# Mixer of a hybrid decoder trunk: low weight parts behind the second norm's root, forget gate's products and fold apart, norm product and one copy moved

## The chip, the cores and the metric

The kernel runs on one core of one Trainium2 chip. The metric is the device time of one execution in microseconds (us), the median of several runs. The core has five engines with a queue of instructions each: TensorE (PE, matrix products, with its weight loads shown as PEld), VectorE (DVE), ScalarE (ACT), GpSimd (POOL) and SyncE (SP, which here issues the DMAs of the weights). An engine works its queue in order; an instruction that waits holds up what is behind it.

## The reference

Two layers, each of three sub-layers with a residual: a SwiGLU, a token mixer, a SwiGLU. Each is preceded by an RMS norm that is shifted and scaled by a condition `c`. The mixer projects 256 tokens of width 1024 to the inputs of three mixers, which run side by side:

```python
def _mixer(h, w_in, b_fgate, ...):
    proj = h @ w_in
    (lru_x, lru_g, sb_q, sb_k, sb_v, fx_q, fx_k, fx_v, fx_f) = jnp.split(proj, SPLIT_POINTS, axis=-1)
    u = _causal_depthwise_conv(lru_x, conv_w, conv_b)
    y_lru = _rg_lru(u, ...) * jax.nn.gelu(lru_g)
    y_sb = _stick_breaking_attention(...sb_q, sb_k, sb_v...)
    fq = _rms(...fx_q...) * g_qk[0]
    fk = _rms(...fx_k...) * g_qk[1]
    log_f = jax.nn.log_sigmoid(fx_f.astype(jnp.float32) + b_fgate.astype(jnp.float32))
    y_fox = _forgetting_attention(fq, fk, ...fx_v..., log_f.transpose(0, 2, 1))
    y = jnp.concatenate([_rms(y_lru), _rms(y_sb), _rms(y_fox)], axis=-1) * g_mix_out
    return y @ w_out

for l in range(DEPTH):
    x = x + 0.5 * gate(0) * _swiglu(norm_mod(x, 0), w_ffn_up[l, 0], w_ffn_down[l, 0])
    x = x + gate(1) * _mixer(norm_mod(x, 1), w_in[l], ...)
    x = x + 0.5 * gate(2) * _swiglu(norm_mod(x, 2), w_ffn_up[l, 1], w_ffn_down[l, 1])
```

## The kernel before

The 256 tokens are two tiles, t = 0 and 1, of 128. A product in float32 is made of three products of a reduced format (fp32r): every operand is split into a high part (`H`, `hTh`, `gh`) and a low part (`L`, `hTl`, `gl`), and high x high, high x low and low x high are summed in PSUM. A weight unit of 128x1024 is loaded by SP into a buffer `raw` (six of them), ACT casts it to `H`, and DVE subtracts to get `L`; `H` and `L` share a pool of eleven pairs. `unit(key)` starts this when a unit is first asked for, so load, cast and subtraction stand in the queues around the product that asks first, or ahead of it.

A Tile scheduler sets the order within each engine's queue from the order of the program, its priorities and its dependencies. Two constructs steer it: `tc.issue_after(ins)` keeps an instruction behind another, and `tc.high_priority()` lets it go as early as that allows. So a change at one place moves instructions elsewhere too.

Norm: ACT squares x and sums (`junk`, L396), DVE takes the root with seven small instructions on 128x1 (`v` L399, `ny`, `na` in `rsqrt`, L359 to L364), ACT scales x with it (`xn`, L407), PE transposes (`tp`, L418), ACT and DVE shift and scale (`hf`), and the split follows (`hTh`, `hTl`). The second norm is that of tile t = 1.

The mixer's projection has five groups of 512 columns: LG (the gelu's input), LX (the conv's), FX (q and k of the forgetting attention), SB (q and k of the stick-breaking one) and VV (both values). `proj(g, t)` gives 8 feature tiles k of three matmuls each for one tile of tokens; the matmul of `hTl` of each k is kept in `muls[g, t][k]`. The order is LG t=0, LX t=0, LG t=1, LX t=1, then the gates of the RG-LRU (`go`, after the conv `u` on DVE), FX, SB, VV, and the output products `wo`. The LX result is copied (`lxt`, L634) and transposed (`tx`, L637).

Places that the change touches, beside the split: for FX and t = 1, 16 matmuls `fo` (L677, L678) of all features with the forget gate's weights, a copy `zs` (L680), and two small matmuls `zo` that fold high and low (L683). The copy `qkT` of SB's two results (L771), whose program order is behind the forgetting attention's exponentials `p0` and `p1`. In `group`, the product `mo` (L809) of the RG-LRU's squares `lsq` with ones, for its RMS, which is placed with high priority behind `muls[VV, 0][4]`. `ada_step` slips units of the conditioning's product into the mixer of the first layer (L292, L317, DVE).

Of the kernel before, what the change touches and what calls it, by code (L numbers as in the profile page):

```python
# [9 lines left out]
F32 = mybir.dt.float32  # L10
# [3 lines left out]
AF = mybir.ActivationFunctionType  # L14
ALU = mybir.AluOpType
# [5 lines left out]
KT = D // 128  # L21
# [4 lines left out]
NT = SEQ // 128  # L26
# [3 lines left out]
LX, LG, SB, FX, VV = range(5)  # L30
# [64 lines left out]
def trunk_kernel(ctx: ExitStack, tc: tile.TileContext, x, c, wst, ada, par, cst, row, wg, out):  # L95
# [32 lines left out]
    V, A, T, S = nc.vector, nc.scalar, nc.tensor, nc.sync  # L128
# [35 lines left out]
    def C(name):  # L164
        o, n = CST[name]
        return c_sb[:, o:o + n]
# [11 lines left out]
    for n in range(2):  # L178
        q = slice(n * 512, (n + 1) * 512)
        o = PT([128, 512], name="pc")  # L180
# [50 lines left out]
        T.matmul(o, start=False, stop=True, skip_group_check=True, **k)  # L231


    live = {}


    norm_end, hold = {}, []

    def held(engine):
        return tc.issue_after(norm_end[engine].ins) if hold and engine in norm_end else nullcontext()  # L240

    def split(raw):
        h = hlp.tile([128, 1024], F32R, tag="H", name="H")
        lo = hlp.tile([128, 1024], F32R, tag="L", name="L")
        with held("A"):
            A.copy(h, raw)  # L246
        V.tensor_tensor(out=lo, in0=raw, in1=h.bitcast(F32), op=ALU.subtract)  # L247
        return h, lo

    def unit(key):  # L250
        if key not in live:
            raw = rawp.tile([128, 1024], F32, tag="raw", name="raw")
            S.dma_start(out=raw, in_=wst[W_UNITS[key]])
            live[key] = split(raw)
        return live[key]
# [6 lines left out]
    def over_features(o, t, w, mid=None, by=4):  # L262

        hh, hl = hT[t]
        muls = []
        for k0 in range(0, KT, by):
            for k in range(k0, k0 + by):
                for i, part in enumerate(w(k)):  # L270
                    T.matmul(o, lhsT=hh[:, k, :], rhs=part, start=k == 0 and i == 0, stop=False)  # L271
            for k in range(k0, k0 + by):
                mul = T.matmul(o, lhsT=hl[:, k, :], rhs=w(k)[0], start=False, stop=k == KT - 1)  # L273
                muls.append(mul)
                if mid and mid[0] == k:
                    mid[1](mul)
        return muls
# [62 lines left out]
    def ada_step(n):  # L340
        for _ in range(n):
            if ada_todo:
                f, a = ada_todo[-1]
                if f is ada_gate and a[2] == 0:
                    if not gate_free[a[1] % 2]:
                        return
                    gate_free[a[1] % 2] = False
                ada_todo.pop()
                f(*a)
# [6 lines left out]
    def rsqrt(v, n, name):  # L356
        y = SM([128, n], name=name + "y")
        a = SM([128, n], name=name + "a")
        V.tensor_scalar(out=y.bitcast(I32), in0=v.bitcast(I32), scalar1=-0.5, scalar2=float(0x5F1FFFF9),  # L359
                        op0=ALU.mult, op1=ALU.add)  # L360
        for c in (-2.38924456, -3.0 / NEWTON ** 2):
            if n == 1:
                V.tensor_scalar(out=a, in0=y, scalar1=v, scalar2=y, op0=ALU.mult, op1=ALU.mult)
                V.tensor_scalar(out=y, in0=a, scalar1=c, scalar2=y, op0=ALU.add, op1=ALU.mult)  # L364
            else:
                V.tensor_tensor(out=a, in0=y, in1=y, op=ALU.mult)
                V.tensor_tensor(out=a, in0=a, in1=v, op=ALU.mult)
                V.scalar_tensor_tensor(out=y, in0=a, scalar=c, in1=y, op0=ALU.add, op1=ALU.mult)
        return y


    hTh = const.tile([128, NT, KT, 128], F32R, name="hTh")
    hTl = const.tile([128, NT, KT, 128], F32R, name="hTl")
# [211 lines left out]
    def mixer(l, after):  # L585
        wgt = W4([128, 2, 4, 128], name="wgt")
        S.dma_start(out=wgt, in_=wg[l])
        wfs = const.tile([128, KT, 8], F32R, name="wfs", tag="wfs")
# [4 lines left out]
        muls = {}  # L593

        def proj(g, t):
            o = PA([128, 512], name="pj")

            def w(k):
                q = slice((k % 2) * 512, (k % 2 + 1) * 512)
                return [part[:, q] for part in unit(("in", l, g, k // 2))]  # L600

            muls[g, t] = over_features(o, t, w, (K_T[2], flush) if (g, t) == (LX, 0) else None, by=1)
            ada_step(ADA_MIX[l] if g in (FX, VV) else 0)
            return o

        def proj_w(g, b):

            o = PA([128, 2, SEQ], name="pj")
            with ExitStack() as behind:
                for k in range(KT):  # L610
                    wh, wl = unit(("in", l, g, k // 2))
                    for h, w in ((0, wh), (0, wl), (1, wh)):
                        for i in range(2):
                            q = (k % 2) * 512 + (2 * b + i) * 128
                            opens = k == 0 and h == 0 and w is wh and i == 0
                            mul = T.matmul(o[:, i], lhsT=w[:, q:q + 128], rhs=(hTh, hTl)[h][:, :, k, :], start=opens,  # L616
                                           stop=True, skip_group_check=True)
                            if opens:
                                behind.enter_context(tc.issue_after(mul.ins))
            ada_step(ADA_MIX[l])  # L620
            return o

        def behind(mul):
            return tc.issue_after(mul.ins)
# [24 lines left out]
        if True:  # L649
            for f2, hf in enumerate(halves):  # L650
                for f in (2 * f2, 2 * f2 + 1):
                    A.activation(u[:, f, :], xT[:, f, 3:3 + SEQ], AF.Identity,
                                 scale=cw[:, 3 * 4 + f:3 * 4 + f + 1], bias=cbias[:, f:f + 1])
# [4 lines left out]
                for gi, (dst, b) in enumerate(((rg, P(f"br{l}")), (ig, P(f"bi{l}")))):  # L658
                    o = PD([128, 2, SEQ], name="go")
# [11 lines left out]
        for t in range(NT):  # L671
            o = proj(FX, t)
            if t == 1:
                z4 = SM([128, NT, 4], name="z4")
                fo = PT([8, NT, 128], name="fo")
                for k in range(KT):
                    T.matmul(fo, lhsT=wfs[:, k, :], rhs=hTh[:, :, k, :], start=k == 0, stop=False)  # L677
                    T.matmul(fo, lhsT=wfs[:, k, :], rhs=hTl[:, :, k, :], start=False, stop=k == KT - 1)  # L678
                zs = W2([8, NT, 128], name="zs")
                A.copy(zs, fo)  # L680
                zo = PT([128, NT, 4], name="zo")
                for t in range(NT):
                    T.matmul(zo[:, t, :], lhsT=zs[:, t, :], rhs=C("fold")[0:8, :], start=True, stop=True)  # L683
                V.tensor_tensor(out=z4, in0=zo, in1=R(f"bf{l}").unsqueeze(1).to_broadcast([128, NT, 4]), op=ALU.add)
                z4 = z4.rearrange("p t h -> p (t h)")
            o3 = o.rearrange("p (h d) -> p h d", d=HD)
            sq = W2([128, 8, HD], name="fsq")
            A.activation(sq, o3, AF.Square)
            s8 = SM([128, 8], name="s8")
            V.tensor_reduce(out=s8, in_=sq, axis=AX.X, op=ALU.add)  # L690

            r8 = SM([128, 8], name="r8")
            act(r8[:, 0:4], s8[:, 0:4], AF.Ln, bias=eps64_t)
            act(r8[:, 4:8], s8[:, 4:8], AF.Ln, scale=1.0 / HD, bias=eps_t)
            act(r8, r8, AF.Exp, scale=-0.5)
            V.tensor_tensor(out=qa[t][:, :, 0:HD], in0=o3,
                            in1=r8.unsqueeze(2).to_broadcast([128, 8, HD]), op=ALU.mult)
            for i in range(2):
                V.tensor_tensor(out=qa[t][:, 4 * i:4 * i + 4, 0:HD], in0=qa[t][:, 4 * i:4 * i + 4, 0:HD],
                                in1=R(f"gqk{l}")[:, i * HD:(i + 1) * HD].unsqueeze(1).to_broadcast([128, 4, HD]),  # L700
                                op=ALU.mult)
            V.memset(qa[t][:, 0:4, 65:66], 1.0)
            V.memset(qa[t][:, 4:8, 64:65], 1.0)
# [64 lines left out]

        qkT = W4([128, 4, SEQ], name="qkT")
        for b in range(2):  # L770
            A.activation(qkT[:, 2 * b:2 * b + 2, :], proj_w(SB, b), AF.Copy, scale=(0.125, 1.0)[b])  # L771


        gm = P(f"gm{l}")
# [26 lines left out]
        def group(y, sq, out, at=None):  # L801

            n = out.shape[1]
            mo = PT([128, SEQ], name="mo")
            with ExitStack() as place:
                if at:
                    place.enter_context(tc.high_priority())
                    place.enter_context(behind(at))
                T.matmul(mo, lhsT=ones_r.bitcast(F32), rhs=sq, start=True, stop=True)  # L809
            rl = W2([128, SEQ], name="rl")  # L810
            act(rl, mo, AF.Ln, scale=1.0 / (128 * n), bias=eps_t)
            act(rl, rl, AF.Exp, scale=-0.5)
            V.tensor_tensor(out=out, in0=y, in1=rl.unsqueeze(1).to_broadcast([128, n, SEQ]), op=ALU.mult)
# [3 lines left out]
        vt = W4([128, 2, 512], name="vt")  # L817
        for t in range(NT):
            A.copy(vt[:, t], proj(VV, t))
        group(hs, lsq, hs, muls[VV, 0][4])  # L820
        split(0, 4, hs)


# [256 lines left out]
```

## Time and profile before

| | us |
|---|---|
| median of 3 runs | 1004.42 (1003.95 to 1005.36) |
| the profiled execution | 1003.98 |
| its span | 1001.8 |
| PE busy | 978.9 |
| DVE busy | 761.7 |
| ACT busy | 531.9 |
| first mixer, 200 to 325 us: PE, DVE, ACT busy | 116.91, 104.86, 86.80 |
| second mixer, 697 to 810 us: PE, DVE, ACT busy | 111.19, 80.02, 84.48 |

A row of a timeline gives the start, the busy time, the engine, the line, the operation, output<-input, the shape, the count, and in brackets the idle time before it and what ended that. A row of waits gives who waited for whom, the sum, the count and the longest. A row of windows gives a stretch, its length, busy time (and instructions) of PE, PEld, DVE, ACT and POOL, then the granted clock of PE, the busy share of the DMA engines and GB/s.

### The profile page before, as it was taken

How to read it: one execution, taken by the hardware profiler on the slowest of the kernel's cores; microseconds unless marked ns; L12 is line 12 of the kernel's file. 1: busy time of each engine (PE TensorE's matmuls, PEld its weight loads, DVE VectorE, ACT ScalarE, POOL GpSimd, SP SyncE). 2: the span in 40 equal slices, each digit the busy share in tenths (PEclk: the TensorE clock that was granted, in tenths of full speed). 3: DMA queues.
4: the chain of work that ended last, by engine and by line, in shares of the span. 5: the costliest groups of instructions: out<-in, count | busy, mean ns of one | idle time of the engine just before them, and what ended most of it. 6: DMA issues, size and time to landing. Idle time of an engine off the chain costs nothing.

```text
span 1001.8 us, 15817 instructions
## 1 busy us (share of the span) xinstructions
PE 978.9 (98%) x6054; PEld 857.9 (86%) x6054; DVE 761.7 (76%) x1224; ACT 531.9 (53%) x854; POOL 6.9 (1%) x16
## 2 busy tenths in 40 slices
PE   6999999989899999999999999999999999999998
PEld 4999999867867899999888999997788778999996
DVE  8998888689896998788589878755778679646352
ACT  5374435568675535354364434545678755535340
POOL 0000000000000000000000000000000000000000
PEclk9999999999999999999999999999999999999999
DMA  8999989677673799889639999955452339746511
GB/s 315 356 331 347 348 333 342 212 250 262 218 226 121 235 376 368 310 333 341 243 120 343 358 354 333 327 184 182 165 195 89 106 125 351 278 171 207 172 64 42
DMA packets 69965, 251.26 MB, mean 251 GB/s; under 512 B 8065, under 2 KB 8705, under 8 KB 69890
## 3 DMA queue, kind: packets, MB, share of 16 engines
q1 hardware_dynamic: 68834, 247.09, 69.3%
q0 software_dynamic: 1056, 3.17, 0.9%
q8 instruction: 47, 0.77, 0.3%
q14 instruction: 28, 0.23, 0.1%
HBM read 249.16 MB, written 1.07 MB: 250 GB/s over the span
## 4 chain that ended last, share of the span: by engine, by line
PE 91%; DVE 4%; ACT 2%; DMA 1%; issue 1%; ACTq 0%; DVEq 0%
PE up L470 39%; PE dn L258 8%; PE dn L260 8%; PE dn L259 8%; PE up L271 8%; PE up L273 4%; PE pj L271 4%; PE pj L616 2%; PE pj L273 2%; PE wo L258 1%; PE wo L259 1%; PE wo L260 1%; DVE L L247 1%; DMA raw<-in_wst 1%; PE tp L418 1%
## 5 line engine op out<-in xcount | busy, mean ns | idle before, releaser
L247 DVE TENSOR_TENSOR L<-raw,H 128x1024 fp32r<-128x1024 f32 x320 | 382.1, 1221 | 78.0 <-ACT H L246 76.9
L246 ACT CAST H<-raw 128x1024 fp32r<-128x1024 f32 x320 | 328.8, 1052 | 90.9 <-DMA raw<-in_wst 44.3
L470 PE MATMUL up<-hTh,H 128*128 128x256 f32 x1088 | 211.2, 281 | 1.9 <-ACT H L246 1.9
L470 PE MATMUL up<-hTl,H 128*128 128x256 f32 x1088 | 209.7, 281 | 0.0
L470 PE MATMUL up<-hTh,L 128*128 128x256 f32 x1088 | 208.7, 279 | 0.0
L470 PEld LDWEIGHTS up<-hTh,H 128*128 128x128 f32 x1088 | 168.4, 189 | 8.6 <-ACT H L246 2.3
L470 PEld LDWEIGHTS up<-hTl,H 128*128 128x128 f32 x1088 | 163.9, 188 | 0.0
L470 PEld LDWEIGHTS up<-hTh,L 128*128 128x128 f32 x1088 | 163.1, 188 | 0.0
L462 ACT ACTIVATE sg<-up 128x256 f32<-128x256 f32 x88 | 33.8, 384 | 232.0 <-PE up L470 200.2
L258 PE MATMUL dn<-H,gh 128*128 128x512 f32 x352 | 139.9, 398 | 0.4 <-ACT gh L535 0.4
L260 PE MATMUL dn<-H,gl 128*128 128x512 f32 x352 | 139.8, 397 | 0.0
L259 PE MATMUL dn<-L,gh 128*128 128x512 f32 x352 | 138.8, 394 | 0.0
L292 DVE SCALAR_TENSOR_TENSOR raw<-raw,cb 128x1024 f32<-128x1024 f32 x96 | 114.3, 1220 | 1.0 <-DMA raw<-in_ada 0.8
L260 PEld LDWEIGHTS dn<-H,gl 128*128 128x128 f32 x352 | 66.1, 188 | 15.9 <-DVE gl L536 0.6
L258 PEld LDWEIGHTS dn<-H,gh 128*128 128x128 f32 x352 | 66.2, 188 | 13.5 <-ACT gh L535 1.7
L259 PEld LDWEIGHTS dn<-L,gh 128*128 128x128 f32 x352 | 66.2, 188 | 12.6
L519 DVE TENSOR_TENSOR sg<-sg,up 128x256 f32<-128x256 f32 x68 | 28.5, 420 | 62.3 <-ACT sg L462 62.0
L271 PE MATMUL up<-H,hTh 128*128 128x512 f32 x160 | 64.1, 401 | 0.6 <-DVE hTh L431 0.6
L271 PE MATMUL up<-L,hTh 128*128 128x512 f32 x160 | 63.6, 398 | 0.0
L273 PE MATMUL up<-H,hTl 128*128 128x512 f32 x160 | 57.7, 397 | 0.0
L317 DVE SCALAR_TENSOR_TENSOR raw<-raw,cb 128x1024 f32<-128x1024 f32 x48 | 56.8, 1220 | 1.2 <-DMA raw<-in_ada 1.1
L271 PE MATMUL pj<-H,hTh 128*128 128x512 f32 x128 | 53.0, 414 | 1.6 <-ACT qkT L771 1.6
(229 smaller groups left out, 1053.1 us busy)
## 6 DMA issues: line engine op xcount, KB each, us to landing
raw<-in_wst SPq DMA_DIRECT2D x320, 512.0 KB, 5.3
raw<-in_ada SPq DMA_DIRECT2D x144, 512.0 KB, 5.3
gate<-row POOLq DMA_DIRECT2D x6, 512.0 KB, 6.7
x<-in_x SPq DMA_DIRECT2D x2, 512.0 KB, 4.0
wgt<-in_wg SPq DMA_DIRECT2D x2, 512.0 KB, 6.0
out_x<-x SPq DMA_DIRECT2D x4, 256.0 KB, 2.0
once<-in_cst SPq DMA_DIRECT2D x1, 192.0 KB, 5.8
p_sb<-in_par SPq DMA_DIRECT2D x1, 168.0 KB, 5.2
```

What stands on the lines that cost most here:

```text
L246: A.copy(h, raw)
L247: V.tensor_tensor(out=lo, in0=raw, in1=h.bitcast(F32), op=ALU.subtract)
L258: T.matmul(o, lhsT=xh, rhs=wh, start=first, stop=False)
L259: T.matmul(o, lhsT=xh, rhs=wl, start=False, stop=False)
L260: return T.matmul(o, lhsT=xl, rhs=wh, start=False, stop=last)
L271: T.matmul(o, lhsT=hh[:, k, :], rhs=part, start=k == 0 and i == 0, stop=False)
L273: mul = T.matmul(o, lhsT=hl[:, k, :], rhs=w(k)[0], start=False, stop=k == KT - 1)
L292: V.scalar_tensor_tensor(out=raw, in0=raw, scalar=1.0, in1=cb, op0=ALU.mult, op1=ALU.mult, accum_out=st[:, v, k:k + 1])
L317: V.scalar_tensor_tensor(out=raw, in0=raw, scalar=1.0, in1=cb, op0=ALU.mult, op1=ALU.mult, accum_out=col[:, k:k + 1])
L462: used.append(A.activation(*a, **k))
L470: return T.matmul(o[:, v], lhsT=w[:, q:q + 128], rhs=(hTh, hTl)[h][:, :, k, :], start=opens, stop=True, skip_group_check=True)
L519: V.tensor_tensor(out=sg, in0=sg, in1=o[:, 1], op=ALU.mult)
```

## The change

Four edits. While `proj(LX, 0)` is built, from feature tile 2 on, the `L` of a unit that is asked for is issued behind the last instruction of the root that was built last, that of the second norm (three units: LX's second to fourth). `fo` is placed with high priority behind `muls[FX, 1][2]`, `zo` behind `muls[FX, 1][7]`. `qkT`'s copies get high priority. `mo` of the RG-LRU goes behind `muls[VV, 0][7]`.

```diff
+    last = {}
+    rooted = []
...
-        V.tensor_tensor(out=lo, in0=raw, in1=h.bitcast(F32), op=ALU.subtract)
+        with tc.issue_after(last["root"].ins) if rooted else nullcontext():
+            V.tensor_tensor(out=lo, in0=raw, in1=h.bitcast(F32), op=ALU.subtract)
...
-                V.tensor_scalar(out=y, in0=a, scalar1=c, scalar2=y, op0=ALU.add, op1=ALU.mult)
+                last["root"] = V.tensor_scalar(out=y, in0=a, scalar1=c, scalar2=y, op0=ALU.add, op1=ALU.mult)
...
+                if (g, t) == (LX, 0) and k == 2:
+                    rooted.append(1)
                 return [part[:, q] for part in unit(("in", l, g, k // 2))]
             muls[g, t] = over_features(o, t, w, (K_T[2], flush) if (g, t) == (LX, 0) else None, by=1)
+            rooted.clear()
...
-                for k in range(KT):
-                    T.matmul(fo, lhsT=wfs[:, k, :], rhs=hTh[:, :, k, :], start=k == 0, stop=False)
-                    T.matmul(fo, lhsT=wfs[:, k, :], rhs=hTl[:, :, k, :], start=False, stop=k == KT - 1)
+                with tc.high_priority(), behind(muls[FX, 1][2]):
+                    for k in range(KT):
+                        T.matmul(fo, lhsT=wfs[:, k, :], rhs=hTh[:, :, k, :], start=k == 0, stop=False)
+                        T.matmul(fo, lhsT=wfs[:, k, :], rhs=hTl[:, :, k, :], start=False, stop=k == KT - 1)
...
-                for t in range(NT):
-                    T.matmul(zo[:, t, :], lhsT=zs[:, t, :], rhs=C("fold")[0:8, :], start=True, stop=True)
+                with behind(muls[FX, 1][7]):
+                    for i in range(NT):
+                        T.matmul(zo[:, i, :], lhsT=zs[:, i, :], rhs=C("fold")[0:8, :], start=True, stop=True)
...
-            A.activation(qkT[:, 2 * b:2 * b + 2, :], proj_w(SB, b), AF.Copy, scale=(0.125, 1.0)[b])
+            o = proj_w(SB, b)
+            with tc.high_priority():
+                A.activation(qkT[:, 2 * b:2 * b + 2, :], o, AF.Copy, scale=(0.125, 1.0)[b])
...
-        group(hs, lsq, hs, muls[VV, 0][4])
+        group(hs, lsq, hs, muls[VV, 0][7])
```

What becomes of it in the queues, in the first layer. The number behind a name is that of the tile, the same in both kernels; the lines of the changed kernel are its own.

DVE at the second norm's root, before (`v_2331`, `ny_2333` and `na_2334` are the root's values):

```order
L247 TENSOR_TENSOR L_2467<-raw_2464,H_2466 128x1024
L399 TENSOR_TENSOR v_2331<-ss_2326 128x1
L247 TENSOR_TENSOR L_2596<-raw_2593,H_2595 128x1024
L359 TENSOR_SCALAR ny_2333<-v_2331 128x1
L247 TENSOR_TENSOR L_2608<-raw_2605,H_2607 128x1024
L363 TENSOR_SCALAR na_2334<-ny_2333,v_2331 128x1
L247 TENSOR_TENSOR L_2620<-raw_2617,H_2619 128x1024
L364 TENSOR_SCALAR ny_2333<-na_2334,ny_2333 128x1
L317 SCALAR_TENSOR_TENSOR raw_2641,gt01_2085<-raw_2641,cb_92 128x1024
L363 TENSOR_SCALAR na_2334<-ny_2333,v_2331 128x1
L317 SCALAR_TENSOR_TENSOR raw_2644,gt01_2085<-raw_2644,cb_92 128x1024
L364 TENSOR_SCALAR ny_2333<-na_2334,ny_2333 128x1
```

The same place now:

```order
L451 TENSOR_TENSOR x1_89<-x1_89,tmp_2323 128x512
L405 TENSOR_TENSOR v_2331<-ss_2326 128x1
L365 TENSOR_SCALAR ny_2333<-v_2331 128x1
L369 TENSOR_SCALAR na_2334<-ny_2333,v_2331 128x1
L370 TENSOR_SCALAR ny_2333<-na_2334,ny_2333 128x1
L369 TENSOR_SCALAR na_2334<-ny_2333,v_2331 128x1
L370 TENSOR_SCALAR ny_2333<-na_2334,ny_2333 128x1
L253 TENSOR_TENSOR L_2419<-raw_2416,H_2418 128x1024
L638 MEMSET xT_2349 128x4x3
L253 TENSOR_TENSOR L_2431<-raw_2428,H_2430 128x1024
L253 TENSOR_TENSOR L_2467<-raw_2464,H_2466 128x1024
L253 TENSOR_TENSOR L_2596<-raw_2593,H_2595 128x1024
```

The root's instructions stand together, directly behind the residual; `L_2419`, `L_2431` and `L_2467` (LX's second to fourth unit; the first two stood some 15 rows ahead of the root) and all that was between the root's instructions come behind it.

On ACT, ahead of the first norm's `xn` in the same layer, before:

```order
L457 ACT_TABLE_LOAD
L246 CAST H_2430<-raw_2428 128x1024
L407 ACTIVATE xn_2261<-x0_88,ny_2227 128x512 x2
L535 CAST gh_2268<-tg_2265 128x256
L426 ACTIVATE hf_2289<-tp_2284,S01_1345,G01_1344 128x128 x4
```

and now:

```order
L463 ACT_TABLE_LOAD
L413 ACTIVATE xn_2261<-x0_88,ny_2227 128x512 x2
L541 CAST gh_2268<-tg_2265 128x256
L251 CAST H_2430<-raw_2428 128x1024
L432 ACTIVATE hf_2289<-tp_2284,S01_1345,G01_1344 128x128 x4
```

The cast of LX's third unit went behind `xn` and `gh`.

On PE, at the end of the first layer's mixer (`wo` are the output products, `tp` the transposes of the next norm's first tile), before:

```order
L260 MATMUL wo_3201<-H_3315,hTl_138 128x512
L418 MATMUL tp_3417<-c_sb_94,xn_3348 128x128 x4
L418 MATMUL tp_3429<-c_sb_94,xn_3348 128x128 x4
L258 MATMUL wo_3202<-H_3306,hTh_137 128x512
L259 MATMUL wo_3202<-L_3307,hTh_137 128x512
L260 MATMUL wo_3202<-H_3306,hTl_138 128x512
L258 MATMUL wo_3202<-H_3315,hTh_137 128x512
L259 MATMUL wo_3202<-L_3316,hTh_137 128x512
```

and now:

```order
L266 MATMUL wo_3201<-H_3315,hTl_138 128x512
L264 MATMUL wo_3202<-H_3306,hTh_137 128x512
L265 MATMUL wo_3202<-L_3307,hTh_137 128x512
L266 MATMUL wo_3202<-H_3306,hTl_138 128x512
L264 MATMUL wo_3202<-H_3315,hTh_137 128x512
L265 MATMUL wo_3202<-L_3316,hTh_137 128x512
L424 MATMUL tp_3417<-c_sb_94,xn_3348 128x128 x4
L266 MATMUL wo_3202<-H_3315,hTl_138 128x512
L424 MATMUL tp_3429<-c_sb_94,xn_3348 128x128 x4
L277 MATMUL up_3470<-H_3473,hTh_137 128x512
```

The transposes went behind five of the last six output products; ahead of `up` of the next SwiGLU only one is left between and behind them. Elsewhere on PE, the second norm's transposes `tp` come after 15 of LX's 24 matmuls (before: after all), `tx` after two more matmuls of LG t=1, and `mo` after 26 VV matmuls (before: 21). On ACT, the two copies `qkT` stand behind the first and the second of the four `p1` (before: behind all four), and one cast that stood ahead of the four stands behind them.

## The prediction

> **What bounds the kernel now.** I read the page's busy times first, then the waits of TensorE alone, once over each token mixer, then the timelines around each wait.
>
> ```profile
> PE 978.9 (98%) x6054; PEld 857.9 (86%) x6054; DVE 761.7 (76%) x1224; ACT 531.9 (53%) x854; POOL 6.9 (1%) x16
> ```
>
> TensorE (PE) is busy for 98% of the span of 1001.8 us, so the change can only win what PE loses. The diff touches the two mixers; these are PE's waits in the first (200 to 325 us) and the second (697 to 810 us):
>
> ```profile
> PE tx L637 <- ACT lxt L634: 2.0, 1, 2.0
> PE pj L271 <- ACT qkT L771: 1.6, 1, 1.6
> PE mo L809 <- DVE lsq L798: 1.5, 1, 1.5
> PE zo L683 <- ACT zs L680: 1.0, 1, 1.0
> PE tp L418 <- ACT xn L407: 0.9, 2, 0.5
> PE go L662 <- DVE u L655: 0.6, 1, 0.6
> PE up L271 <- DVE hTh L431: 0.3, 1, 0.3
> PE dn L258 <- ACT gh L535: 0.2, 1, 0.2
> ```
>
> ```profile
> PE tx L637 <- ACT lxt L634: 0.8, 1, 0.8
> PE tp L418 <- ACT xn L407: 0.5, 1, 0.5
> PE dn L258 <- ACT gh L535: 0.2, 1, 0.2
> ```
>
> Each row gives who waited for what, the sum, how often and the longest. The first mixer loses 8.1 us in waits, the second 1.5 at the places that the change reaches. One more loss stands in no wait: matmuls that ran slowly.
>
> ```profile
> 218.82 0.66 PE L418 MATMUL tp<-c_sb,xn 128*128 128x128 f32 x4 [0.43 <-ACT xn L407]
> ...
> 222.10 1.11 PE L637 MATMUL tx<-c_sb,lxt 128*128 128x128 f32 x4 [2.00 <-ACT lxt L634]
> 222.87 0.78 PE L271 MATMUL pj<-H,hTh 128*128 128x512 f32 x1
> ...
> 224.72 0.46 PE L271 MATMUL pj<-H,hTh 128*128 128x512 f32 x1
> 225.02 0.39 PE L271 MATMUL pj<-L,hTh 128*128 128x512 f32 x1
> 225.25 0.39 PE L273 MATMUL pj<-H,hTl 128*128 128x512 f32 x1
> ```
>
> ```profile
> 235.98 0.62 PE L637 MATMUL tx<-c_sb,lxt 128*128 128x128 f32 x4
> 236.35 0.48 PE L271 MATMUL pj<-L,hTh 128*128 128x512 f32 x1
> ```
>
> ```profile
> 220.00:230.00 10.00, 8.00 (x32) 6.51 (x32) 6.38 (x13) 6.54 (x12) 0.00 (x0) 0.83 0.61 243
> ```
>
> From 222.87 to 224.72 four matmuls went by, 0.46 each, where the steady pitch is 0.23 (225.02 to 225.25): 0.93 too much. The four transposes before them took 0.77, the same four 0.37 at 235.98: 0.40 more. The granted clock (the number before the last two) is 0.83 in these 10 us. So the tx place costs 0.43 + 2.00 + 1.33 = 3.76 us.
>
> VectorE (DVE) is close behind: between the second norm and the norm product `mo` it is busy for 65.55 of 73.21 us, so it has 7.66 idle.
>
> ```profile
> 210.36:283.57 73.21, 66.33 (x367) 53.86 (x365) 65.55 (x116) 47.46 (x97) 1.09 (x2) 0.98 0.70 245
> ```
>
> **The change part by part.** No instruction is added or removed; everything is order.
>
> *Low parts behind the root.* Before, the seven small instructions of the second norm's root alternate with large ones:
>
> ```profile
> 211.49 0.16 DVE L399 TENSOR_TENSOR v<-ss 128x1 f32<-128x1 f32 x1
> 211.56 1.22 DVE L247 TENSOR_TENSOR L<-raw,H 128x1024 fp32r<-128x1024 f32 x1
> ...
> 217.80 0.21 DVE L364 TENSOR_SCALAR ny<-na,ny 128x1 f32<-128x1 f32 x1
> ```
>
> ```profile
> 316.88 0.16 DVE L399 TENSOR_TENSOR v<-ss 128x1 f32<-128x1 f32 x1 [0.85 <-ACT junk L396]
> ...
> 318.13 0.21 DVE L364 TENSOR_SCALAR ny<-na,ny 128x1 f32<-128x1 f32 x1
> ```
>
> The chain takes 6.52 us (211.49 to 218.01) there, and 1.46 where nothing stands between (316.88 to 318.34). In the new order it stands alone, so it ends about 5 us sooner, at 212.4, if its sums come no later than now. On ACT, `xn` and then the first `lxt` copy follow it:
>
> ```profile
> 218.05 1.34 ACT L407 ACTIVATE xn<-x,ny 128x512 f32<-128x512 f32 x2 [6.77 <-DVE ny L364]
> ...
> 221.44 0.61 ACT L634 COPY lxt<-pj 128x512 f32<-128x512 f32 x1
> ```
>
> PE's transposes `tp` now come nine LX matmuls earlier and `tx` two matmuls after LX: the waits of 0.43 and 2.00 and the slow stretch lose their cause. Two smaller waits take their place. First, `L` of the second LX unit can start only at 212.4 and takes 1.14 to the next start: 213.5. PE needs it after 24 LG and 7 LX matmuls:
>
> ```profile
> 207.03 0.40 PE L271 MATMUL pj<-H,hTh 128*128 128x512 f32 x1
> ```
>
> That is the first LG matmul; it comes 0.7 to 1.0 sooner (next part), and 31 times the pitch of 0.23 is 7.1, so the need is at 213.1 to 213.4: I count 0.3 as lost. Second, `tx` still waits for a copy of 0.61 beside two matmuls of 0.23: at most 0.3 seen. I take 3.76 - 0.6 = **3.16 gained** (ends: 0 if the two waits just change names, 3.76). The gate's four products, which stood in the chain, and the weight loads that reuse their buffers come some 6 us later; FX and SB, which use them, start over 15 us later. That cover would have to shrink by 9 us to cost anything.
>
> *The copies ahead of the first `xn`.* The new order puts one cast behind it:
>
> ```profile
> 201.10 1.05 ACT L246 CAST H<-raw 128x1024 fp32r<-128x1024 f32 x1
> 202.06 1.33 ACT L407 ACTIVATE xn<-x,ny 128x512 f32<-128x512 f32 x2
> 203.30 0.35 ACT L535 CAST gh<-tg 128x256 fp32r<-128x256 f32 x1
> ```
>
> `xn` and `gh` come 0.96 sooner (201.10 to 202.06), against PE's two waits of 0.49 and 0.21: **0.70 gained** in layer 0 (ends 0 and 1.0). The displaced `H` is for the third LX unit, needed 9 us later.
>
> *`go`.* Its wait of 0.63 ends with `u`, at the end of a DVE chain behind the second `tx`. PE and that chain come earlier by about the same 4 us. I leave 0.2 for the pairs after the first: **0.43 gained** (ends -0.5, 0.63).
>
> *`fo` and `zo` apart.* Now `zs` is copied behind a cast that waited for its load:
>
> ```profile
> 254.44 1.05 ACT L246 CAST H<-raw 128x1024 fp32r<-128x1024 f32 x1 [0.56 <-DMA raw<-in_wst]
> ```
>
> In the new order some 15 matmuls of FX stand between `fo` and `zo`, 3.5 us for a copy of 0.36. The wait of 0.96 goes. ACT has two casts ahead of `qaT` instead, whose loads may be late: 0.1. **0.86 gained** (ends 0, 0.96).
>
> *`qkT` ahead of the softmax's end.* PE's wait of 1.61 (at 274.80) is for this copy, behind the last exponentials:
>
> ```profile
> 273.69 0.48 ACT L462 ACTIVATE p<-s,mx 128x256 f32<-128x256 f32 x1
> ...
> 274.14 0.61 ACT L771 ACTIVATE qkT<-pj 128x512 f32<-128x512 f32 x1
> ```
>
> It now goes ahead of three of four such pieces, and a cast that stood ahead of the four moves behind them: 3 x 0.45 + 1.05 = 2.4 sooner on ACT, against PE's wait of 1.61. I take all **1.61 gained** (ends 0.9, 1.61, since ACT waits for the scores too). The three pieces it overtakes are needed only by the later products with the values.
>
> *`mo` later.* PE has 26 instead of 21 VV matmuls ahead of it, 5 x 0.23 = 1.17. PE arrived there at 282.32 (283.80 less 1.48). With the 6.76 of the parts above it arrives at 282.32 - 6.76 + 1.17 = 276.7. `lsq` is DVE's: two gate products of 1.22 fewer stand ahead of it, so if DVE stays as idle as now, it comes 2.44 sooner, at 281.36; if all 7.66 idle goes, at 273.7. Half of the idle is spent waiting for the chains that get shorter; I take the middle, 277.5. The wait is then 0.8 instead of 1.48: **0.68 gained** (ends -3.2, 1.48).
>
> *The end of the mixer.* Here the new order is worse. Before, the next norm's transposes stood ahead of the last two sets of output matmuls; now five of those six are ahead of the first `tp`:
>
> ```profile
> 321.18 1.03 PE L418 MATMUL tp<-c_sb,xn 128*128 128x128 f32 x8
> 321.97 0.48 PE L258 MATMUL wo<-H,hTh 128*128 128x512 f32 x1
> ...
> 323.90 0.50 PE L271 MATMUL up<-H,hTh 128*128 128x512 f32 x1 [0.28 <-DVE hTh L431]
> ```
>
> The chain from `tp` to `up` took 2.72 (321.18 to 323.90), with six matmuls of 0.23 beside it. With one beside it 5 x 0.23 = 1.17 come into the open: **-1.2** (ends -1.2, 0, the latter if `xn` has come late in either order).
>
> *Layer 1.* The same two moves ahead of its mixer: 0.71 for `xn` and `gh`, 0.76 for `tx`, less 0.3 for the `L` behind the root: **1.17 gained** (ends -1, 1.5). Its `tp` at the end stays where it was.
>
> Sum: 3.16 + 0.70 + 0.43 + 0.86 + 1.61 + 0.68 - 1.2 + 1.17 = 7.4. The profiled execution took 1003.98 us, span 1001.8 and 2.2 around it; the runs' median is 1004.42, so it is an ordinary one. 1003.98 - 7.4 = **996.6**.
>
> On the slow stretch: in the Trainium skill, "TensorE: Matmul & The Clock Gate", Part 1, says that the clock falls to half after an idle window of about 3.4 us, and Part 4 that transposes do not count as busy in the same way. The trace has a pitch of 0.46 against 0.23, and nothing but transposes and waits for 4.05 us (218.82 to 222.87), while a wait of 1.61 alone left the clock at 1.00 in its 10 us, so it agrees:
>
> ```profile
> 270.00:280.00 10.00, 8.39 (x60) 6.66 (x59) 10.00 (x16) 8.71 (x20) 0.00 (x0) 1.00 0.50 157
> ```
>
> By that page the 1.33 goes, since matmuls now stand between the transposes; if instead the stretch returned elsewhere, the sum would be 997.9.
>
> **The rivals.**
> - *DVE keeps its idle time.* It is busy for 90% of the stretch up to `mo`, and its idle time comes from ACT and DMA as much as from PE. Then `lsq` comes at 281.36, PE waits 4.6 there instead of 0.8: 3.8 less, **1000.4**. For it: DVE is in order. Against it: DVE's largest gap, 3.62 us idle in 220 to 230, lies behind the root chain.
> - *All the waits go.* No loss at the end, `mo` free: 8.1 + 1.33 + 1.5 = 10.9, **993.1**.
> - *Slower: the `L`s behind a late root.* Behind the first of them DVE holds every later `L`, so LX's third to eighth feature tiles wait for the root. Each us of the root past 212.1 costs PE one, in both layers. To undo 7.4 and lose 2 more it must be 4.7 late twice; at 5 us it is **1006.6**. The root's sums come from ACT, where each cast of 1.05 in front would delay them; against it, ACT stood idle for 6.77 there.
> - *Nothing changes.* The waits only swap owners (`tx` for `L`, `zo` for `qaT`, `qkT` for `mo`), with the end's 1.2 against the 1.4 of the first `xn` in both layers: about **1003.8**.
>
> **How the numbers follow.** My forecast 0.50, DVE's idle time 0.20, all waits gone 0.13, nothing 0.09, late root 0.08. The likeliest's own range is 994 to 999. The range reaches down to 992.8 and up to 1002.0, over the first three. About 0.2% (2 us) is what a measurement of this kernel can tell from no change: faster below 1002.4, slower above 1006.4. Faster takes the first three, 0.83; same 0.10; slower 0.07.
>
> **What would show it.** In the new profile: the root within 1.5 us, `xn` near 212.5, no wait at `tx` over 0.4 and no slow matmul behind it; no wait at `zo` and at the first VV matmul; a wait at `mo` under 1.5; one of about 1.5 at `up` after the first mixer. Wrong would be a wait of PE for `L` over 1 us in LX, or of over 3 us at `mo`.

## The result

The changed kernel takes 998.23 us (median of 4 runs, 997.53 to 998.76), the kernel before 1004.18 (4 runs on the same chip): ratio 0.9938, 95% interval 0.992 to 0.9956. That is 5.95 us less; the forecast was 7.4 less.

PE's waits in the first mixer, from the view of waits of the changed kernel (195 to 320 us; who waited for whom, sum, count, longest):

```profile
PE mo L822 <- DVE lsq L811: 1.7, 1, 1.7
PE up L277 <- DVE hTh L437: 1.5, 1, 1.5
PE tf L733 <- ACT qaT L735: 1.1, 1, 1.1
PE tx L646 <- ACT lxt L643: 0.5, 2, 0.3
```

and in the second (690 to 805 us):

```profile
PE up L277 <- DVE hTh L437: 0.3, 1, 0.3
PE tx L646 <- ACT lxt L643: 0.2, 1, 0.2
```

Gone are the waits at `tp`, `dn`, `go`, `zo` and at the first VV matmul, and all but 0.5 at `tx`. One at `tf` is new, one at `up` has grown, and `mo` waits as before (1.7, it was 1.5). The root's timeline on DVE:

```profile
210.61 0.16 DVE L405 TENSOR_TENSOR v<-ss 128x1 f32<-128x1 f32 x1 [1.05 <-ACT junk L402]
...
211.87 0.21 DVE L370 TENSOR_SCALAR ny<-na,ny 128x1 f32<-128x1 f32 x1
212.00 2.36 DVE L253 TENSOR_TENSOR L<-raw,H 128x1024 fp32r<-128x1024 f32 x2
```

The chain takes 1.47 us (210.61 to 212.08) instead of 6.52, and ends at 212.1; DVE stands idle for 1.05 ahead of it, since the low parts that filled this place now come behind it. `xn` starts at 212.12, `tx` waits 0.21:

```profile
219.06 0.65 PE L646 MATMUL tx<-c_sb,lxt 128*128 128x128 f32 x4 [0.21 <-ACT lxt L643]
219.47 0.48 PE L279 MATMUL pj<-H,hTl 128*128 128x512 f32 x1
219.78 0.39 PE L277 MATMUL pj<-H,hTh 128*128 128x512 f32 x1
```

No slow matmul follows. At the end of the first mixer PE waits for what comes behind `tp`:

```profile
315.30 0.66 PE L424 MATMUL tp<-c_sb,xn 128*128 128x128 f32 x4
315.71 0.48 PE L266 MATMUL wo<-H,hTl 128*128 128x512 f32 x1
316.03 0.60 PE L424 MATMUL tp<-c_sb,xn 128*128 128x128 f32 x4
318.11 0.50 PE L277 MATMUL up<-H,hTh 128*128 128x512 f32 x1 [1.48 <-DVE hTh L437]
```

Waits do not show all that PE loses, so the table below counts it otherwise: in each stretch, the start-to-start time of all PE matmuls less a steady pitch (0.2335 us for 512 columns, 0.1175 for 256, 0.11 for smaller). The zero is arbitrary; differences between kernels are what counts. "VV" is the start of the matmuls for VV, "norm" the next norm's first transpose; L0 and L1 are the two layers, and their first columns start at the end of the SwiGLU ahead of the mixer. All runs of the experiments are in it, each by one execution.

| PE's loss, us | L0 to go | go to VV | VV to mo | mo to norm | norm to up | L1 to mo | L1 mo to up | sum |
|---|---|---|---|---|---|---|---|---|
| before | 6.28 | 6.35 | 1.76 | 2.28 | 0.55 | 5.66 | 1.53 | 24.4 |
| changed | 1.24 | 4.16 | 2.00 | 2.23 | 1.81 | 4.06 | 2.99 | 18.5 |
| e1 root undone | 5.85 | 3.77 | 0.05 | 2.46 | 0.55 | 5.46 | 2.95 | 21.1 |
| e2 root alone | 1.53 | 5.17 | 1.80 | 2.15 | 1.33 | 4.01 | 1.57 | 17.6 |
| e3 copy undone | 1.05 | 4.85 | 0.62 | 2.06 | 0.55 | 4.02 | 3.01 | 16.2 |
| e4 mo undone | 0.77 | 4.86 | 2.02 | 2.21 | 1.80 | 4.38 | 1.54 | 17.6 |
| e5 products together | 0.90 | 4.17 | 2.00 | 1.47 | 1.81 | 4.04 | 2.19 | 16.6 |
| e6 casts behind qaT | 1.08 | 3.93 | 0.58 | 1.80 | 0.58 | 4.04 | 2.99 | 15.0 |
| e7 lsq ahead | 1.24 | 4.09 | 0.46 | 2.00 | 2.00 | 4.05 | 3.04 | 16.9 |
| e8 gate undone | 1.22 | 4.16 | 2.00 | 2.22 | 1.81 | 4.15 | 2.97 | 18.5 |
| e9 four edits and three | 0.74 | 3.93 | 0.58 | 1.44 | 0.55 | 3.99 | 2.18 | 13.4 |
| e10 root, gate and three | 0.93 | 5.29 | 1.52 | 1.67 | 0.59 | 4.87 | 1.56 | 16.4 |

Before to changed: 24.4 less 18.5 is 5.9, the 5.95 of the runs. Layer 0 gives 5.8 of it, layer 1 only 0.14: its mixer wins 1.60 up to `mo` and loses 1.46 behind it, in a stretch where the view of waits shows nothing new. There the timeline of PE shows, before and after:

```profile
779.77 0.60 PE L873 MATMUL tpp<-c_sb,p 128*128 128x128 f32 x4
780.30 1.08 PE L885 MATMUL yfx<-pa,vt 128*64 128x256 f32 x8
781.31 0.50 PE L259 MATMUL wo<-L,hTh 128*128 128x512 f32 x1
```

```profile
774.33 1.08 PE L898 MATMUL yfx<-pa,vt 128*64 128x256 f32 x6
775.33 0.39 PE L231 MATMUL zb<-gh,ntri_r 128*128 128x256 f32 x1
775.65 0.65 PE L898 MATMUL yfx<-pa,vt 128*64 128x256 f32 x2
776.22 0.50 PE L265 MATMUL wo<-L,hTh 128*128 128x512 f32 x1
```

The four products of the values with the softmax's weights (each is two records in the trace, on 64 of the 128 columns) took 1.01 together (780.30 to 781.31). Now three take 1.00, as long as four did, and the fourth 0.57 by itself, behind `zb`.

### The profile page after: what moved, and what is told of

Same layout as the page of the kernel before. It is cut to its first block, busy times and chain, and to the rows that moved or that the text cites. A ratio compares the mean times of both kernels' runs of the same rounds, so it can differ in the third digit from the quotient of the medians.

```text
span 996.1 us, 15802 instructions
## 1 busy us (share of the span) xinstructions
PE 977.7 (98%) x6054; PEld 856.0 (86%) x6054; DVE 762.1 (77%) x1224; ACT 531.8 (53%) x854; POOL 6.9 (1%) x16
## 4 chain that ended last, share of the span: by engine, by line
PE 90%; DVE 6%; DMA 2%; ACT 1%; issue 1%; DVEq 0%; ACTq 0%
PE up L476 37%; PE dn L266 8%; PE dn L264 8%; PE dn L265 8%; PE up L277 8%; PE pj L277 4%; PE up L279 4%; PE pj L279 2%; PE wo L265 2%; PE wo L264 2%; PE wo L266 1%; DVE L L253 1%; DVE raw L298 1%; DMA raw<-in_wst 1%; PE pj L625 1%; PE tp L424 1%
```

## The experiments

Theories: **A**, PE waited for the root's chain, and what goes there is won. **B**, DVE's work sets the first mixer; what is won ahead of `mo` is lost at `mo`. **C**, layer 1's tail lost its time to the separated fourth product. Three more, D to F, came with the runs. e1 to e4, e5 to e7 and e8 to e10 ran together, beside 1002.84, 1003.65 and 1003.8 us of the kernel before; e1 to e8 are one execution each, and eleven executions of the kernel before lay between 1001.95 and 1007.15 us, so tenths are read from the table.

**e1, the root undone**

```diff
-        with tc.issue_after(last["root"].ins) if rooted else nullcontext():
+        with nullcontext():
             V.tensor_tensor(out=lo, in0=raw, in1=h.bitcast(F32), op=ALU.subtract)
```

> The changed kernel with the low parts free to go ahead of the root again; the other three edits stay. Theory A (the root's chain on DVE is what PE waited for at tp and tx): the wait of about 2.0 us at tx, the slow matmuls behind it, and the waits at the first xn of both layers come back, and the transposes at the end of the first mixer go back ahead of the output products, so that the 1.5 us at up falls to 0.3. Loss up to zo 6 us in layer 0 (from 3.2 to about 9), 1.5 in layer 1; the wait of 1.7 at mo shrinks to under 0.5, the 1.1 at tf goes: 1001.5 to 1003.5 us. Theory B (DVE's total work ahead of mo sets the first mixer, so what is won ahead of it is lost at mo): the wait at mo vanishes and the time is within 1.5 us of the changed kernel's: 997 to 999.7.

Measured 1000.47 us, 2.4 under the kernel before. Neither theory held alone. The waits at `tp` and `tx` came back, theory A's half (the first two columns go from 5.40 to 9.62, and layer 1 loses 1.40 more up to `mo`), but `mo` waits for nothing now (2.00 to 0.05) and the transposes at the end are back (1.81 to 0.55). Put on top of the three other edits, the root wins 5.6 us of loss in two layers and gives 3.2 back, at `mo` and at the end of the first mixer. Without it, the three others are worth 3.3 (24.4 to 21.1). The slow stretch came back too, behind a wait of the same length, with a granted clock of 0.83 in the window of 220 to 230 us:

```profile
222.31 0.66 PE L646 MATMUL tx<-c_sb,lxt 128*128 128x128 f32 x4 [2.01 <-ACT lxt L643]
...
223.51 0.63 PE L277 MATMUL pj<-H,hTh 128*128 128x512 f32 x1
223.94 0.63 PE L279 MATMUL pj<-H,hTl 128*128 128x512 f32 x1
224.37 0.63 PE L277 MATMUL pj<-H,hTh 128*128 128x512 f32 x1
```

**e2, the root alone**: the three other edits are taken back. Against the kernel before, this is left:

```diff
-        V.tensor_tensor(out=lo, in0=raw, in1=h.bitcast(F32), op=ALU.subtract)
+        with tc.issue_after(last["root"].ins) if rooted else nullcontext():
+            V.tensor_tensor(out=lo, in0=raw, in1=h.bitcast(F32), op=ALU.subtract)
...
-                V.tensor_scalar(out=y, in0=a, scalar1=c, scalar2=y, op0=ALU.add, op1=ALU.mult)
+                last["root"] = V.tensor_scalar(out=y, in0=a, scalar1=c, scalar2=y, op0=ALU.add, op1=ALU.mult)
...
+                if (g, t) == (LX, 0) and k == 2:
+                    rooted.append(1)
...
+            rooted.clear()
```

> The kernel before with only the low parts put behind the root. Theory A: waits at tp and tx as in the changed kernel (tx at most 0.4), the waits at zo and at the first VV matmul stay at about 1.0 and 1.6 (or move to mo): gain 3.5 to 5 us against the kernel before, 999.2 to 1000.7. Theory B: the gain is spent at zo, qkT and mo, whose waits grow by what came earlier: gain under 2 us, above 1002.2. By theory C (the loss of 1.4 us in the second mixer's tail comes from the four products yfx, of which one was separated from its neighbours by the place of mo) the tail of layer 1 is as in the kernel before, since the four stand together here: 1.3 us lost from mo to the next norm, not 2.6.

Measured 997.11 us, 5.7 under the kernel before and below what theory A expected; by the table 6.8 less is lost, a little more than by all four edits. There is no wait at `zo`, and the one at the first VV matmul is 0.6, without the edits made for them: the casts ahead of `zs` no longer wait for their loads, and the cast that stood ahead of the four `p1` now stands behind `qkT`. The tail of layer 1 is as before (1.57), as theory C has it.

**e3, the copy undone**

```diff
-            with tc.high_priority():
+            with nullcontext():
                 A.activation(qkT[:, 2 * b:2 * b + 2, :], o, AF.Copy, scale=(0.125, 1.0)[b])
```

> The changed kernel without the high priority of qkT's copies. Theory A: PE waits 1.0 to 1.6 us for qkT at the first VV matmul again, and the wait at mo falls by the same (DVE sets when lsq is ready, not PE), so that nothing is lost by it; the transposes at the end of the first mixer stand ahead of six products again, so that the 1.5 us at up falls to 0.3: 996.5 to 997.8, faster than the changed kernel. Rival: qkT's copy was worth its 1.6 us by itself, PE's arrival at mo sets what follows: 998.5 to 999.5.

Measured 995.35 us, 7.5 under the kernel before: better than with the edit. PE loses 0.69 more up to VV, of which 0.6 is a wait for `qkT`, and 1.38 less at `mo`; and with the transposes back ahead of six products, 1.26 less at `up`. The rival, that the copy is worth its 1.6 us, fell. `mo` gained twice what theory A gave it: the order on DVE changed too, with one low part fewer in front of `lsq` (see e7).

**e4, mo undone**

```diff
-        group(hs, lsq, hs, muls[VV, 0][7])
+        group(hs, lsq, hs, muls[VV, 0][4])
```

> The changed kernel with mo back behind muls[VV, 0][4]. In layer 0 mo keeps its place in PE's queue, so layer 0 keeps its time. In layer 1 the four products yfx stand together again. Theory C (separating the fourth of them cost 0.57 for the products and 0.20 for the product put between them): the tail of layer 1 loses 1.3 to 1.9 us instead of 2.6: 996.8 to 997.6. Rival (the tail lost time to alternating kinds of matmul everywhere, not to that pair): unchanged within 0.3 us, 998.

Measured 996.95 us. In layer 0 the order on PE, ACT and DVE is that of the changed kernel, `mo`'s place included, so its differences (0.5 less up to `go`, 0.7 more up to VV, where it waited 1.8 at `tf` instead of 1.1) show how far two executions of one order can differ in a stretch. Layer 1's tail loses 1.54 instead of 2.99, and 0.32 more up to `mo`: this edit costs 1.1 us, in layer 1.

**e5, the products together**

```diff
-                        with behind(opened[e]) if e in opened else nullcontext():
+                        with tc.high_priority() if opened else nullcontext(), behind(opened[e]) if e in opened else nullcontext():
                             mul = T.matmul(y[64 * e:64 * e + 64, p, 128 * part:SEQ], lhsT=v, rhs=w,
```

> The changed kernel, with the products with the values (yfx, ysb) at high priority once their first has gone, so that the four yfx stand together in both layers. All else in PE's queue up to there is the same. Theory C: each separated fourth costs 0.57 for the products and about 0.20 for what stands between: 0.6 to 0.8 us off the stretch from mo to the next norm in each layer, loss there from 2.2 and 2.4 to about 1.5 and 1.7; 1.2 to 1.6 us less than the changed kernel in all. Rival (the tail loses to alternation between kinds of matmul, wherever): less than 0.3 in each.

Measured 995.92 us. Theory C holds for this product: 0.76 less from `mo` to the norm in layer 0, 0.80 in layer 1. PE's timeline in layer 1:

```profile
773.13 1.08 PE L898 MATMUL yfx<-pa,vt 128*64 128x256 f32 x8
774.15 0.38 PE L231 MATMUL zb<-gh,ntri_r 128*128 128x256 f32 x1
774.37 0.39 PE L265 MATMUL wo<-L,hTh 128*128 128x512 f32 x1
```

Products and `zb` take 1.24 (773.13 to 774.37) instead of 1.89 (774.33 to 776.22): 0.65 of the 0.80. So the separated product explains 0.65 to 0.80 of the 1.46 that layer 1's tail lost. e4 gets all of it back with another order of the small products, so the rest lies in that order too; which of its changes it is was not tested.

**e6, the casts behind qaT.** Theory **D**: on ACT, `qaT` stood behind a cast that waited for its load. The changed kernel's ACT:

```profile
251.39 0.44 ACT L468 ACTIVATE e<-e 128x8 f32<-128x8 f32 x2
256.25 1.05 ACT L251 CAST H<-raw 128x1024 fp32r<-128x1024 f32 x1 [4.42 <-DMA raw<-in_wst]
257.20 0.57 ACT L735 COPY qaT<-tf 66x512 f32<-66x512 f32 x1
257.68 1.04 ACT L251 CAST H<-raw 128x1024 fp32r<-128x1024 f32 x1
258.63 0.58 ACT L735 COPY qaT<-tf 66x512 f32<-66x512 f32 x1
```

ACT was held for 4.42 us, of which PE paid only the last 1.09, since the operands of `qaT` were not there earlier; SP's queue shows why the load was late, before and after:

```profile
236.56 10.32 SPq L290 DMA_DIRECT2D raw<-in_ada  x4
248.27 12.28 SPq L253 DMA_DIRECT2D raw<-in_wst  x8
```

```profile
243.62 4.94 SPq L296 DMA_DIRECT2D raw<-in_ada  x4
250.15 8.58 SPq L259 DMA_DIRECT2D raw<-in_wst  x5
```

The four loads of the conditioning go out 7 us later, and the weights' loads behind them 2 us later.

```diff
-    def split(raw):
+    def split(raw, key=None):
...
-        with held("A"):
-            A.copy(h, raw)
+        early = key[0] == "out" and WO.index(key[2]) < 2
+        with tc.high_priority() if early else nullcontext(), tc.issue_after(last["qaT"].ins) if early else nullcontext():
+            with held("A"):
+                A.copy(h, raw)
...
-            live[key] = split(raw)
+            live[key] = split(raw, key)
...
-                    A.copy(dst[:, :, t * 128:(t + 1) * 128], tp)
+                    last["qaT"] = A.copy(dst[:, :, t * 128:(t + 1) * 128], tp)
```

> The changed kernel with the casts of the first two output units behind qaT's copies on ACT. Theory D (ACT sits in the queue before a cast whose load lands late, since the gate's products, moved behind the root, free the load buffers late; qaT waits behind it): the wait of 1.1 us at tf falls to 0.2 or less. What it gives then meets mo: if DVE sets lsq, the wait at mo grows by the same 0.9 and the time stays within 0.5 us of the changed kernel's; if not, 0.9 less. Rival: qaT waits for its own transposes or for DVE; the wait at tf stays near 1.1.

Measured 995.25 us. The wait at `tf` is gone, as theory D has it; but one of 0.6 for `qkT` is back at the first VV matmul, so only 0.23 less is lost up to VV. What was expected of `mo` was wrong: its wait went as well (its column falls from 2.00 to 0.58), where theory B had it grow. DVE shows why:

```profile
273.14 1.22 DVE L255 TENSOR_TENSOR L<-raw,H 128x1024 fp32r<-128x1024 f32 x1
274.27 0.68 DVE L813 TENSOR_TENSOR lsq<-lsq 128x512 f32<-128x512 f32 x1
274.88 1.22 DVE L255 TENSOR_TENSOR L<-raw,H 128x1024 fp32r<-128x1024 f32 x1
276.01 0.42 DVE L813 TENSOR_TENSOR lsq<-lsq 128x256 f32<-128x256 f32 x1
```

From the first instruction of the second norm's root to the end of `lsq` (276.43 us here, 277.82 in the changed kernel, shown under e7) DVE takes 64.95 us instead of 67.21. It is idle for 2.65 of them instead of 3.85: its copy `kaT`, which had waited 1.04 for the late `tf`, no longer does. And one low part of 1.14 fewer stands there (19 instead of 20). So about half of the win at `mo` came through the end of the wait for `qaT`, and half by another order on DVE. The end is back at 0.58, since this order, too, puts `tp` ahead of most of the last products.

**e7, lsq ahead**

```diff
-    def split(raw):
+    def split(raw, key=None):
...
-        with tc.issue_after(last["root"].ins) if rooted else nullcontext():
+        after = last["root"] if rooted else last["lsq"] if key[0] == "out" and WO.index(key[2]) >= 2 else None
+        with tc.issue_after(after.ins) if after else nullcontext():
             V.tensor_tensor(out=lo, in0=raw, in1=h.bitcast(F32), op=ALU.subtract)
...
-            live[key] = split(raw)
+            live[key] = split(raw, key)
...
-                V.tensor_tensor(out=sq[:, 0:n, :], in0=sq[:, 0:n, :], in1=sq[:, n:2 * n, :], op=ALU.add)
+                add = V.tensor_tensor(out=sq[:, 0:n, :], in0=sq[:, 0:n, :], in1=sq[:, n:2 * n, :], op=ALU.add)
+            last.setdefault((l, "lsq"), add)
+            last["lsq"] = last[l, "lsq"]
```

> The changed kernel with the low parts of the third to eighth output unit behind lsq's last addition on DVE (three of them, 3.5 us, stood ahead of it in layer 0). Theory E (lsq is late only because DVE's queue has these low parts ahead of it): the wait at mo in layer 0 falls from 1.7 to under 0.3, and 1.0 to 1.7 us go; the next norm's transposes are behind all six products here, so the wait at up is about 1.7. Theory B (DVE's work in all bounds the mixer): the products wo wait for the low parts instead, and the time stays within 0.4 us of the changed kernel's.

Measured 996.64 us. The wait at `mo` is 0.2, and 1.65 us of loss go in layer 0: theory E. In the changed kernel DVE has three low parts in front of and between `lsq`'s two additions (273.40 to 277.41):

```profile
273.40 2.35 DVE L253 TENSOR_TENSOR L<-raw,H 128x1024 fp32r<-128x1024 f32 x2
275.67 0.68 DVE L811 TENSOR_TENSOR lsq<-lsq 128x512 f32<-128x512 f32 x1
276.27 1.22 DVE L253 TENSOR_TENSOR L<-raw,H 128x1024 fp32r<-128x1024 f32 x1
277.41 0.41 DVE L811 TENSOR_TENSOR lsq<-lsq 128x256 f32<-128x256 f32 x1
```

The other traces agree: from the end of the scan to the end of `lsq` DVE works without a gap for 8.5 us with four low parts in that stretch (the changed kernel, e4, e5, e8, e10), and for 7.3 to 7.5 with three (e3, e6, e9), where the wait at `mo` is 0.3 or none. So what stood in front of `lsq` on DVE, a wait (e6) and low parts (e6, e7), set `mo`, and not the sum of DVE's work; theory B falls.

**e8, the gate undone**: `fo` and `zo` together behind FX, as before.

```diff
-                with tc.high_priority(), behind(muls[FX, 1][2]):
-                    for k in range(KT):
+                for k in range(KT):
...
-                with behind(muls[FX, 1][7]):
-                    for i in range(NT):
+                for t in range(NT):
...
```

> The changed kernel with the forget gate's 16 products and their fold back together behind FX. Theory A (fo and zo had to be moved apart, since zs is copied behind a cast): PE waits about 0.9 us at zo again, loss from go to zo and on to the first VV matmul up by that. Theory F (with the root early, the load in front of zs has landed by then, as root alone showed no wait at zo): no wait over 0.2 at zo, time within 0.4 us of the changed kernel's.

Measured 998.7 us, with the same loss as the changed kernel in every stretch (18.5), and no wait at `zo`: theory F. This edit is worth nothing once the root is early.

**e9 and e10, the best of the parts.** e9 has all four edits, e5's and e6's, and the last six products held behind the transposes:

```diff
-                T.transpose(tp[:, i, :], xn[:, k * 128:(k + 1) * 128], ident)
+                turned["tp"] = T.transpose(tp[:, i, :], xn[:, k * 128:(k + 1) * 128], ident)
...
-                for m in WO[-2:]:
-                    w_out(m, t, [n])
+                with behind(turned["tp"]) if t == 1 and n == 1 else nullcontext():
+                    for m in WO[-2:]:
+                        w_out(m, t, [n])
```

> All four edits, and three more: the products with the values together (e5), the casts behind qaT (e6), and the last six output products of the mixer behind the next norm's transposes of the first tile, as in the kernel before. Expected from the parts: loss of layer 0 about 7.2 (e6's 7.96 less 0.7), of layer 1 6.2 (e5): 11.0 us less than the kernel before, ratio 0.989. If the parts share one cause (what DVE can do), less: 0.991 to 0.993.

Measured 993.44 us (median; ratio to the kernel before 0.9892, interval 0.9876 to 0.9909): 10.4 less than before and faster than both kernels (the changed one's interval is 0.992 to 0.9956). The parts add up: the table has 11.0 less lost, as expected.

e10 is e9 without the copy's priority and with `mo` behind `muls[VV, 0][4]`.

> As the one above, but without the priority of qkT's copies and with mo behind muls[VV, 0][4]: only the root and the forget gate's edit, and the three more. If these two edits are worth nothing once ACT is not held up at qaT: within 0.1% of the one above, 0.989; if the copy's lead is worth its 1.6 us: 0.9905.

Measured 996.6 us (0.9922, interval 0.9908 to 0.9937): slower than both expectations. PE waits at the first VV matmul and at `mo`:

```profile
PE pj L279 <- ACT qkT L786: 2.0, 1, 2.0
PE mo L824 <- DVE lsq L813: 1.9, 2, 1.2
```

With ACT no longer held at `qaT`, the copy's lead is worth 1.36 us up to VV, and about 0.9 more is lost between there and `mo` in layer 0, and up to `mo` in layer 1, against 0.6 won behind it; the copy's and `mo`'s shares in that were not separated. In layer 0 four low parts stand ahead of `lsq` again.

## Why the prediction was right, and where not

The direction, the range (992.8 to 1002.0) and the core of the likeliest mechanism, the root's chain, held; the size was 1.4 us too large, the sum of one term that was too small and three that were too large. By its own steps:

- **Root, first `xn`, `go`** (forecast 3.16 + 0.70 + 0.43 = 4.3): 5.0 in the trace (6.28 to 1.24). That the root stands behind it was shown by e1, which loses 4.6 of it again. The wait for `L` behind the root that was counted at 0.3 did not show. The root's end was put at 212.4 without a working (211.49 + 1.46 would be 212.95); it came at 212.1, since the low part ahead of it went too.
- **`zo` and `qkT`** (0.86 + 1.61 = 2.5): 2.2 in the trace. That the size was near is luck, the causes were others: e8 and e2 show that `zo` goes with the root and not with the gate's edit, and in e3 only 0.7 hangs on the copy's priority. 1.1 were paid at `tf`, where 0.1 had been allowed.
- **The gate's products and loads** were put down as covered by 15 us. That step failed: not FX or SB met the later loads, but the weights of the output products, whose cast stood ahead of `qaT` on ACT, and with it `tf` and a part of the wait at `mo` (e6). That the loads are late because the products free their buffers late is argued from SP's queue and not tested.
- **`mo`** (forecast +0.68, from DVE's idle time): -0.24. PE came at 276.26 (forecast 276.7) and `lsq` at 277.82 (277.5); the two small misses make the wait 1.7 and not 0.8, where one under 1.5 had been named as a sign. From the root to `lsq` two gate products fewer stand on DVE, as counted, but 20 low parts instead of 19, which was not; and DVE gave up 2.8 of its 7.66 idle and not the half that was taken, since a new wait of 1.05 stands ahead of the root. The fourth edit does not move `mo` in layer 0 (e4).
- **The end of the mixer** (-1.2): -1.26, as worked out.
- **Layer 1** (1.17): 1.60 up to `mo`, then -1.46 behind it. The sum has no term for the later `mo` there; it changed the order of the small products behind it (e4, e5).
- **The clock**: in the two kernels that wait 2.0 us at `tx` behind the transposes (before and e1) the slow stretch appears, and in the changed kernel it does not. The granted clock before is 0.50 from 221.43 to 224.84 us. PE had nothing but transposes and waits for 4.05 us there, and for 3.7 in e1; in e10 it had the same for 2.98 (eight `tl`, then a wait of 2.0 for `qkT`), and the clock stayed at 1.00. The prediction's wait of 1.61 alone was not alone either: it stood behind eight `tl`, 2.65 us in all. The 1.33 went, as the page of the Trainium skill that the prediction cites ("TensorE: Matmul & The Clock Gate", Part 1 and Part 4) has it: matmuls stand between the transposes now. The wait has shrunk too (2.00 to 0.21), and no run here keeps the one without the other.

Of the rivals, "DVE keeps its idle time" came nearest in time (1000.4), but not in mechanism: DVE's idle time did shrink.

## What to carry to other kernels

A short chain on which another engine waits should not share an in-order queue with long work that nobody needs yet: moving three subtractions was worth 6.8 us of loss, with all that the scheduler reordered by it, and the other three edits, each aimed at a wait that the profile showed, together took 0.9 back on top of it. What an edit is worth hangs on the others: without the root these three won 3.3 (e1), and once `qaT` was freed, two of them were worth 3.2 us (e9 against e10). When a scheduler places the work, read the whole order after an edit: a wait that is shown may go with another edit, and a wait on a load in front of an engine's queue holds up everything behind it. A stretch without waits can still lose time; compare its pitch.

## What the hardware showed that was not expected

Four products on 64 columns each take 1.01 us side by side and 1.57 when the fourth stands alone (1.00 + 0.57), and the matmul between them takes 0.32 (775.33 to 775.65) instead of 0.22 (774.15 to 774.37 in e5): breaking such a group costs more than half of its time, and no engine is shown as waiting. The single records of the traces tell why. In the kernel before the records start in pairs 0.006 to 0.008 us apart (780.297 and 780.303, 780.563 and 780.570, and so on): two products, whose outputs lie in the two halves of the columns, run at once. In the changed kernel the third product has no partner left (774.807, 775.023), so it takes as long as a pair, and the fourth pays that time again.
